# One FFN stage: the order of VectorE's weight-preparing operations within and across steps, and where a chunk's gating writes

## The chip, the cores and the metric

The program runs on one core of one Trainium2 chip. The metric is the device time of one execution in microseconds (us), smaller is better. The engines are named as in the profile: PE (TensorE, matrix products), DVE (VectorE, elementwise), ACT (ScalarE, elementwise and casts), POOL (GpSimd, here mostly the issuer of accumulating DMAs), SP (SyncE, the issuer of the plain loads).

## The reference

One decoder layer on 256 tokens of width 2048, all in float32: a half-weighted SwiGLU FFN, a token mixer, a second half-weighted FFN, a final norm.

```python
def swiglu(h, w_in, w_out):
    gu = h @ w_in
    gate, up = gu[..., :D_FF], gu[..., D_FF:]
    return (jax.nn.silu(gate) * up) @ w_out

h = h + 0.5 * swiglu(rmsnorm(h, ffn1_norm[l]), ffn1_w_in[l], ffn1_w_out[l])
...
h = h + 0.5 * swiglu(rmsnorm(h, ffn2_norm[l]), ffn2_w_in[l], ffn2_w_out[l])
return rmsnorm(h, final_norm)
```

D_FF is 5632. The change touches the two FFNs only; the mixer between them stays.

## The kernel before

**Numbers in two parts.** A float32 operand is held as a rounded part (`hi`, written by an ACT cast, L217) and the remainder (`lo`, written by a DVE subtraction, L220). One product of blocks is then three matmuls, hi x hi, hi x lo and lo x hi (`three`, L300).

**Chunks and steps.** The hidden width is cut into 11 chunks of 512. For each chunk a group of eight steps multiplies the rows by the chunk's gate and up columns; one step covers 256 rows of the weight, 1 MB, in four blocks of 512 columns. A step is of kind S (plain: 8 block products, 24 matmuls) or W (a scheme that trades one product for sums of blocks: 7 products, 21 matmuls). For W, POOL adds one weight block to another by an accumulating DMA (L265), and DVE forms two more sums in the step's own raw tile (`sums`, L273 to L282): the first is 128x512, the second 128x2x512 and needs the first. `KINDS` (L62) gives the kinds by chunk; chunks 3 to 10 are all SWWWWWWW.

**What a W step asks of DVE.** Five operations: the lower part of its three plain blocks (`lo_b`, 128x1536), the first sum (128x512), the second sum (128x1024), and the lower parts of the pairs u and t (`lo_t`, each 128x1024). ACT casts the same parts ahead of each. An S step has one lower part, 128x2048; the first step of a closing group has it as two halves.

**Tiles.** Raw weights lie in a ring of four tiles (three in `ring_raw`, one in `fring_raw` or `zring_raw`); the load of a step waits until the step four before has been read for the last time. Split blocks come from 21 places, 12 for S steps and for the pairs u and t, 9 for the W steps' plain blocks; a place is free again when PE has used it.

**Order.** In `middle` the instructions of DVE, ACT and PE stand in the order in which the program writes them. Its list of phases names, for each step k, what is prepared in which order: casts and load of step k+1 (`hi_b`), lower part of k (`lo_b`), both sums of k, casts of u and t (`hi_t`), lower parts of u and t (`lo_t`). `prepare` runs ahead along this list as far as free places allow, then PE's next unit (half a step) is written. The first chunk of an FFN (`opening`) and the last group (`closing`) are ordered by the framework's scheduler.

**Between chunks.** W products are collected in two PSUM tiles `pw`. At a chunk's end `combine` (L430) turns them into two SBUF tiles `add` by one ACT copy and four DVE operations (L440 to L443). One unit later (`GATE_AT`) `gate` adds them into the chunk's PSUM sums (L628), and forms silu(gate) x up into two buffers of the pool `tmp` (L635 on ACT, L637 on DVE). Two units later (`TURN_AT`) `turned` transposes the result on PE (L648) and splits it (L653, L654). Then a closing group of mostly four S steps, `w_out` times the hidden values of two chunks, runs into PSUM tiles that share their banks with `pw`; `put_away` adds its result to rows in DRAM by POOL DMAs (L685). `x_rows` (L825) loads the input rows for the norm's statistics.

Of the kernel before, what the change touches and what calls it, by code (L numbers as in the profile page):

```python
# [36 lines left out]
P = 128  # L37
# [25 lines left out]
    "f": ("SSSSSSSS", "SSSSSSSS", "WWSWWWSS") + CHUNKS,  # L63
    "z": ("SSSSSSSS", "SWSWWWSS", "WWSWWWSS") + CHUNKS,
# [13 lines left out]
T_BLOCKS = 12  # L78
STRIDE = {"t": 2, "b": 3}
# [7 lines left out]
def layer(ctx: ExitStack, tc: tile.TileContext, io):  # L87
# [7 lines left out]
    tmp = ctx.enter_context(tc.tile_pool(name="tmp", bufs=2))  # L95
# [136 lines left out]
    class Step:  # L232


        def __init__(self, kind, src, halves=False):
            self.kind, self.src, self.halves = kind, src, halves
# [21 lines left out]
        def hi_b(self):  # L258
# [5 lines left out]
            if self.kind == "W":  # L264
                nc.gpsimd.dma_start(  # L265
                    out=self.raw[:, 0, :], in_=self.src[:, CW : 2 * CW], accum_op=ALU.add
                )
            self.hi("b", *((3, "b") if self.kind == "W" else (4, "t")))

        def lo_b(self):  # L270
            self.lo("b")

        def sums(self):  # L273
            if self.kind != "W":
                return
            w = self.raw

            def tt(out, x, y, op):
                nc.vector.tensor_tensor(out=out, in0=x, in1=y, op=op)  # L279
# [4 lines left out]
        def hi_t(self):  # L284
            if self.kind == "W":
                self.hi("u", 2, "t")
                self.hi("t", 2, "t")

        def lo_t(self):
            if self.kind == "W":  # L290
                self.lo("u")
                self.lo("t")
# [284 lines left out]
    def ffn(psum, spool, act, pair, w_in, w_out, row, name, finish, first=None, behind=None):  # L577
# [26 lines left out]
        def opening(c):  # L604
            kinds = KINDS[name][c]
            grp = group(kinds, f"{name}i{c}")
            for i, (kind, kp) in enumerate(pairs_of(c)):
                early = first and c == 0
                if early:
                    act(2 * kp)  # L610
                b = s_step(w_in[c, kp], 4 if early and i == 0 else 2 if early and i == 1 else 1)
                if early:
                    first(kp + 1)
                grp.s(a_of(kp), b)
                if i >= S_AT:
# [5 lines left out]
            a_t = gate(c, grp)  # L621
            turned(c, grp, a_t)

        def gate(c, grp):

            for t in range(NT):
                if grp.with_w:
                    nc.vector.tensor_tensor(  # L628
                        out=grp.acc[t], in0=grp.acc[t], in1=grp.add[t], op=ALU.add
                    )  # L630
            a_t = []
            for t in range(NT):
                r = rstd[0][:, t : t + 1]
                s = tmp.tile([P, CW], F32, tag="sil", name=f"{name}s{c}_{t}")
                nc.scalar.activation(out=s, in_=grp.acc[t][:, 0, :], func=AF.Silu, scale=r)  # L635
                a = tmp.tile([P, CW], F32, tag="act", name=f"{name}a{c}_{t}")
                nc.vector.scalar_tensor_tensor(  # L637
                    out=a, in0=grp.acc[t][:, 1, :], scalar=r, in1=s, op0=ALU.mult, op1=ALU.mult,
                )
                a_t.append(a)  # L640
            return a_t
# [48 lines left out]
        def middle(groups):  # L690

            steps, plan = [], []
            for g in groups:
                if isinstance(g, int):
                    mine = [
                        (Step(kind, w_in[g, kp]), a_of(kp), kp if kind == "W" else None)
# [17 lines left out]
            later = []  # L714

# [22 lines left out]

            k = 0
            for g, mine in plan:  # L740
# [13 lines left out]
                if isinstance(g, int):  # L754
                    def close_up(g=g, grp=grp):
                        a_t = gate(g, grp)
                        later.append([TURN_AT, lambda: turned(g, grp, a_t)])

                    later.append([GATE_AT, close_up])
# [5 lines left out]
        opening(0)  # L765
        with tc.manual_schedule(engines=IN_ORDER):
            grp = middle(GROUPS[1:-1])
# [584 lines left out]
```

## Time and profile before

| | us |
|---|---|
| three runs | 1724.27, 1724.39, 1727.79 |
| median | 1724.39 |
| the profiled execution | 1726.89 |
| its span, first to last instruction | 1725.1 |
| granted clock of PE in it, share of full | 0.996 |

The profile describes one execution. Busy time is listed by engine; matmuls overlap, so their ends are modelled and a busy PE is not PE at its peak. A row of the timeline gives start, length, engine, line, operation, what it writes and reads, its shape and count, and in square brackets idle time of that engine just before and what ended it. A row of the waits gives who waited for whom: us in total, how many times, the longest. A row of the stretches gives the stretch, its length, and for PE, PE's weight loads, DVE, ACT and POOL the busy us with the count of instructions, then the granted clock, the DMA engines' busy share and GB/s.

### The profile page before, as it was taken

To read this page: it belongs to the slowest core of one execution; us is meant where nothing else is said; L and a number is where in the kernel's file an instruction comes from. 1 tells how busy PE (TensorE), PEld (TensorE's weight loads), DVE (VectorE), ACT (ScalarE), POOL (GpSimd) and SP (SyncE) were. 2 spreads that over 40 slices of the span, in tenths; PEclk is the share of its full clock that TensorE was granted. 3 is DMA by queue.
4 is the path that set the end of the run, shared out by engine and by line. 5 is a ranking of instruction groups with operands and counts; after the bars stand their busy time and mean duration, and the time that the engine had idled before them with its cause. 6 is when DMAs were issued, how large, how long until landed. Compare 5 with 4: busy or idle time off the path is not lost. (4 is left out here: it accounts for less than half of the span.)

```text
span 1725.1 us, 21190 instructions
## 1 busy us (share of the span) xinstructions
PE 1686.3 (98%) x7657; PEld 1394.0 (81%) x7657; DVE 1428.5 (83%) x1353; ACT 1011.7 (59%) x1231; POOL 174.6 (10%) x196
## 2 busy tenths in 40 slices
PE   9999999999999999999999999999999999999997
PEld 7888887887887787888988887888878878878876
DVE  8678999999999997645454677889999999999984
ACT  7565566566666564563454555556656666666553
POOL 0010110011011010000000000101101101101112
PEclk9999999999999999999999999999999999999999
DMA  9777897887897796554665666878879878978972
GB/s 347 267 223 235 242 252 236 246 256 237 241 261 236 227 299 222 187 180 140 201 202 180 202 217 174 223 237 243 248 227 256 257 227 240 271 221 254 261 267 93
DMA packets 123387, 398.36 MB, mean 231 GB/s; under 512 B 13825, under 2 KB 17025, under 8 KB 123282
## 3 DMA queue, kind: packets, MB, share of 16 engines
q1 hardware_dynamic: 97026, 335.63, 57.5%
q0 software_dynamic: 25536, 60.30, 18.3%
q8 instruction: 60, 0.98, 0.2%
q10 hardware_dynamic: 720, 1.07, 0.2%
q14 instruction: 45, 0.37, 0.1%
HBM read 371.78 MB, written 25.17 MB: 230 GB/s over the span
## 5 line engine op out<-in xcount | busy, mean ns | idle before, releaser
L217 ACT CAST ring_hi<-ring_raw 128x1024 fp32r<-128x1024 f32 (+3 forms) x558 | 552.4, 1014 | 379.8 <-issue 78.3
L220 DVE TENSOR_TENSOR ring_lo<-ring_raw,ring_hi 128x1024 fp32r<-128x1024 f32 (+5 forms) x443 | 633.7, 1446 | 156.2 <-ACT ring_hi L217 153.6
L279 DVE TENSOR_TENSOR ring_raw<-ring_raw 128x512 f32<-128x512 f32 (+1 forms) x178 | 170.6, 959 | 24.1 <-DMA ring_raw<-in_ffn_w_in 18.4
L303 PE MATMUL ps_fo<-ring_hi,fhi 128*128 128x512 f32 x352 | 138.8, 395 | 9.0 <-DVE add_fi L440 9.0
L265 POOL DMA_DIRECT2D ring_raw<-in_ffn_w_in x89 | 77.1, 866 | 695.8 <-DMA ring_raw<-in_ffn_w_in 349.7
L303 PE MATMUL ps_zo<-ring_hi,zhi 128*128 128x512 f32 x344 | 135.6, 395 | 9.6 <-DVE add_zi L440 9.6
L303 PE MATMUL ps_fo<-ring_hi,flo 128*128 128x512 f32 x352 | 137.2, 390 | 0.0
L303 PE MATMUL ps_fo<-ring_lo,fhi 128*128 128x512 f32 x352 | 137.2, 390 | 0.0
L303 PE MATMUL ps_zo<-ring_hi,zlo 128*128 128x512 f32 x344 | 133.9, 390 | 0.0
L303 PE MATMUL ps_zo<-ring_lo,zhi 128*128 128x512 f32 x344 | 133.8, 389 | 0.0
L303 PE MATMUL pw_zi<-ring_hi,s_z 128*128 128x512 f32 x390 | 131.1, 390 | 1.7 <-DVE zlo L654 1.6
L303 PE MATMUL pw_fi<-ring_hi,s_f 128*128 128x512 f32 x366 | 122.8, 389 | 0.0
L303 PE MATMUL ps_fi<-ring_hi,xT_hi 128*128 128x512 f32 x282 | 109.3, 392 | 2.0 <-ACT ring_hi L217 2.0
L303 PE MATMUL ps_fi<-ring_lo,xT_hi 128*128 128x512 f32 x282 | 110.5, 392 | 0.2 <-DVE ring_lo L220 0.2
L303 PE MATMUL ps_fi<-ring_hi,xT_lo 128*128 128x512 f32 x282 | 110.2, 391 | 0.0
L217 ACT CAST ring_hi<-zring_raw 128x1024 fp32r<-128x1024 f32 x82 | 80.2, 1003 | 38.8 <-DVE zring_raw L279 23.4
L303 PE MATMUL ps_zi<-ring_hi,h_lo 128*128 128x512 f32 x255 | 99.4, 390 | 0.0
L303 PE MATMUL ps_zi<-ring_hi,h_hi 128*128 128x512 f32 x255 | 99.3, 389 | 0.0
L303 PE MATMUL ps_zi<-ring_lo,h_hi 128*128 128x512 f32 x255 | 99.2, 389 | 0.0
L220 DVE TENSOR_TENSOR ring_lo<-zring_raw,ring_hi 128x1024 fp32r<-128x1024 f32 (+2 forms) x60 | 91.8, 1539 | 6.3 <-ACT ring_hi L217 6.2
L217 ACT CAST ring_hi<-fring_raw 128x1024 fp32r<-128x1024 f32 x72 | 71.5, 1015 | 35.2 <-issue 13.4
L220 DVE TENSOR_TENSOR ring_lo<-fring_raw,ring_hi 128x1024 fp32r<-128x1024 f32 (+2 forms) x54 | 81.4, 1518 | 12.2 <-ACT ring_hi L217 11.7
(307 smaller groups left out, 3484.9 us busy)
## 6 DMA issues: line engine op xcount, KB each, us to landing
ring_raw<-in_ffn_w_in SPq DMA_DIRECT2D x262, 512.0 KB, 6.4
ring_raw<-in_ffn_w_out SPq DMA_DIRECT2D x136, 512.0 KB, 5.0
ring_raw<-in_ffn_w_in POOLq DMA_DIRECT2D x89, 256.0 KB, 6.9
fring_raw<-in_ffn_w_in SPq DMA_DIRECT2D x44, 512.0 KB, 6.0
zring_raw<-in_ffn_w_in SPq DMA_DIRECT2D x44, 512.0 KB, 6.2
ring_raw<-in_w_out_mix SPq DMA_DIRECT2D x32, 512.0 KB, 3.8
fring_raw<-in_ffn_w_out SPq DMA_DIRECT2D x20, 512.0 KB, 5.0
zring_raw<-in_ffn_w_out SPq DMA_DIRECT2D x20, 512.0 KB, 4.6
```

What stands on the lines that cost most here:

```text
L217: nc.scalar.copy(out=hi[:, j:k, :], in_=src[:, j:k, :])
L220: nc.vector.tensor_tensor(out=lo, in0=src, in1=hi.bitcast(F32), op=ALU.subtract)
L265: nc.gpsimd.dma_start(out=self.raw[:, 0, :], in_=self.src[:, CW : 2 * CW], accum_op=ALU.add)
L279: nc.vector.tensor_tensor(out=out, in0=x, in1=y, op=op)
L303: nc.tensor.matmul(ps, x, y, start=start and i == 0, stop=stop and i == 2, **kw)
```

## The change

Eight edits, all in the FFN code.

- The phases become a table, `PHASES`: for each k the first sum of k, the cast of u of k, the lower part of t of step k-1, the second sum of k, the cast of t of k, casts and load of step k+2, the lower part `lo_b` of k+1, the lower part of u of k. `sums`, `hi_t` and `lo_t` are split accordingly. The list runs from k = -2. Casts of u and of t now ask for two free places each instead of four at once.
- PE's second unit of a W step is written once both `lo_u` and `lo_t` of it have been.
- `KINDS`: in the first FFN chunk 2 gets six W steps instead of five; in the second FFN chunks 1 and 2 keep four and five in other places.
- `gate` no longer adds into PSUM: it adds PSUM and `add` into `add`, and writes silu and the product over it. A chunk without W steps takes two such tiles anew.
- `opening` returns its group; `middle` gates chunk 0 eight units (first FFN) or one unit (second FFN) into chunk 1 and transposes two units later. Chunk 1 is gated at once instead of one unit later.
- `TMP_BUFS`: the pool `tmp` has one buffer of each tag instead of two.
- `x_rows` puts its rows into the pool `gpool` instead of the `add` tiles.
- `UNSENT` is empty: every W step still uses POOL's accumulating DMA.

```diff
-    "f": ("SSSSSSSS", "SSSSSSSS", "WWSWWWSS") + CHUNKS,
-    "z": ("SSSSSSSS", "SWSWWWSS", "WWSWWWSS") + CHUNKS,
+    "f": ("SSSSSSSS", "SSSSSSSS", "SWWWWWWS") + CHUNKS,
+    "z": ("SSSSSSSS", "SSWWWWSS", "SWWWWWSS") + CHUNKS,
...
+FIRST_GATE_AT = {"f": 8, "z": 1}
+UNSENT = {"f": (), "z": ()}
+TMP_BUFS = 1
+PHASES = (
+    ("sum_u", 0), ("cast_u", 0), ("lo_t", -1), ("sum_t", 0), ("cast_t", 0), ("cast_b", 2),
+    ("lo_b", 1), ("lo_u", 0),
+)
...
-    tmp = ctx.enter_context(tc.tile_pool(name="tmp", bufs=2))
+    tmp = ctx.enter_context(tc.tile_pool(name="tmp", bufs=TMP_BUFS))
...
         def need(self, phase):
-            w = self.kind == "W"
-            return {"hi_b": ("b", 3) if w else ("t", 4), "hi_t": ("t", 4 if w else 0)}.get(phase)
+            if phase == "cast_b":
+                return ("b", 3) if self.kind == "W" else ("t", 4)
+            return ("t", 2) if phase in ("cast_u", "cast_t") else None
...
-            tt(w[:, 2, :], w[:, 0, :], w[:, 2, :], ALU.subtract)
-            tt(w[:, 1:4:2, :], w[:, 1:4:2, :], w[:, 2:3, :].broadcast_to([P, 2, CW]), ALU.subtract)
+            self.less(self.raw[:, 2, :], self.raw[:, 0, :], self.raw[:, 2, :])
...
+            self.less(
+                w[:, 1:4:2, :], w[:, 1:4:2, :], w[:, 2:3, :].broadcast_to([P, 2, CW])
+            )
...
-            for t in range(NT):
-                if grp.with_w:
-                    nc.vector.tensor_tensor(
-                        out=grp.acc[t], in0=grp.acc[t], in1=grp.add[t], op=ALU.add
-                    )
+            if grp.with_w:
+                held = grp.add
+                for t in range(NT):
+                    nc.vector.tensor_tensor(out=held[t], in0=grp.acc[t], in1=held[t], op=ALU.add)
...
-                s = tmp.tile([P, CW], F32, tag="sil", name=f"{name}s{c}_{t}")
-                nc.scalar.activation(out=s, in_=grp.acc[t][:, 0, :], func=AF.Silu, scale=r)
-                a = tmp.tile([P, CW], F32, tag="act", name=f"{name}a{c}_{t}")
+                src = held[t] if grp.with_w else grp.acc[t]
+                s, a = held[t][:, 0, :], held[t][:, 1, :]
+                nc.scalar.activation(out=s, in_=src[:, 0, :], func=AF.Silu, scale=r)
...
-            for k in range(-1, len(steps)):
-                phases += [("hi_b", k + 1), ("lo_b", k), ("sums", k), ("hi_t", k), ("lo_t", k)]
-            phases = [(p, k) for p, k in phases if 0 <= k < len(steps)]
+            for k in range(-2, len(steps) + 1):
+                phases += [(phase, k + ahead) for phase, ahead in PHASES]
+            phases = [
+                (p, k) for p, k in phases
+                if 0 <= k < len(steps) and (steps[k].kind == "W" or p in ("cast_b", "lo_b"))
+            ]
...
-                    prepare(place["lo_t" if i and steps[k].kind == "W" else "lo_b", k])
+                    prepare(max(place[x, k] for x in (("lo_u", "lo_t") if i and steps[k].kind == "W" else ("lo_b",))))
...
+            close_later(0, before, FIRST_GATE_AT[name])
...
-                    later.append([GATE_AT, close_up])
+                    close_later(g, grp, 0 if g == 1 else GATE_AT)
...
-                rows = ftmp[0].tile([P, 2 * CW], F32, tag=f"add{t}", name=f"x_{np_}{t}")
+                rows = gpool.tile([P, 2 * CW], F32, tag=("g_hi", "g_lo")[t], name=f"x_{np_}{t}")
```

Lines move: L220 of before is L227 of the change, L279 is L306, L440 to L443 are L454 to L457, L628 is L642, L637 is L653, L648 is L663, L654 is L669, L303 is L317.

The order on DVE, first place: the second FFN's chunk 10, from the lower part of its second W step's plain blocks on, before. A 128x1536 row is `lo_b`, 128x512 the first sum, 128x2x512 the second, 128x1024 a lower part of u or t; `zring_raw` is the fourth raw tile, here the third W step's.

```order
L220 TENSOR_TENSOR zring_lo<-ring_raw,zring_hi 128x1536
L279 TENSOR_TENSOR ring_raw<-ring_raw 128x512
L279 TENSOR_TENSOR ring_raw<-ring_raw 128x2x512
L220 TENSOR_TENSOR ring_lo<-ring_raw,ring_hi 128x1024 x2
L220 TENSOR_TENSOR ring_lo<-zring_raw,ring_hi 128x1536
L279 TENSOR_TENSOR zring_raw<-zring_raw 128x512
L279 TENSOR_TENSOR zring_raw<-zring_raw 128x2x512
L220 TENSOR_TENSOR ring_lo<-zring_raw,ring_hi 128x1024 x2
```

And in the change:

```order
L227 TENSOR_TENSOR zring_lo<-ring_raw,zring_hi 128x1536
L227 TENSOR_TENSOR ring_lo<-ring_raw,ring_hi 128x1024
L306 TENSOR_TENSOR ring_raw<-ring_raw 128x512
L227 TENSOR_TENSOR ring_lo<-ring_raw,ring_hi 128x1024
L306 TENSOR_TENSOR ring_raw<-ring_raw 128x2x512
L227 TENSOR_TENSOR ring_lo<-zring_raw,ring_hi 128x1536
L227 TENSOR_TENSOR ring_lo<-ring_raw,ring_hi 128x1024
L306 TENSOR_TENSOR zring_raw<-zring_raw 128x512
L227 TENSOR_TENSOR ring_lo<-ring_raw,ring_hi 128x1024
L306 TENSOR_TENSOR zring_raw<-zring_raw 128x2x512
```

Each step's five operations stood together, first sum, second sum, u, t; now a lower part of the step before or after stands between the two sums and ahead of each first sum, and t of a step comes behind the next step's first sum.

Second place, DVE at the end of the same chunk, before: the seventh W step, whose raw tile is `zring_raw`, then the halves of the closing group's first step (from `ring_raw`) and `combine`.

```order
L220 TENSOR_TENSOR zring_lo<-zring_raw,zring_hi 128x1536
L279 TENSOR_TENSOR zring_raw<-zring_raw 128x512
L279 TENSOR_TENSOR zring_raw<-zring_raw 128x2x512
L220 TENSOR_TENSOR ring_lo<-zring_raw,ring_hi 128x1024 x2
L220 TENSOR_TENSOR ring_lo<-ring_raw,ring_hi 128x1024 x2
L440 TENSOR_TENSOR add_zi_1_11341<-pw_zi_0_11126,add_zi_0_11340 128x512
L441 TENSOR_TENSOR add_zi_0_11340<-pw_zi_1_11127,add_zi_1_11341 128x512
```

And in the change, from the lower part of the seventh step's plain blocks on:

```order
L227 TENSOR_TENSOR zring_lo<-zring_raw,zring_hi 128x1536
L227 TENSOR_TENSOR ring_lo<-ring_raw,ring_hi 128x1024
L306 TENSOR_TENSOR zring_raw<-zring_raw 128x512
L227 TENSOR_TENSOR ring_lo<-ring_raw,ring_hi 128x1024
L306 TENSOR_TENSOR zring_raw<-zring_raw 128x2x512
L227 TENSOR_TENSOR ring_lo<-ring_raw,ring_hi 128x1024 x2
L227 TENSOR_TENSOR ring_lo<-zring_raw,ring_hi 128x1024 x2
L454 TENSOR_TENSOR add_zi_1_11267<-pw_zi_0_11050,add_zi_0_11266 128x512
L455 TENSOR_TENSOR add_zi_0_11266<-pw_zi_1_11051,add_zi_1_11267 128x512
```

The two halves of the closing group's first step (the two rows of 128x1024 from `ring_raw` ahead of the last pair) stood behind the seventh step's u and t, and now stand ahead of them; `combine` follows the same set of operations in both.

Third place, PE in the second FFN's chunk 1, from the last transposes of chunk 0 (`ztp`) to the first matmul into the second `pw` tile (`pw_zi_1`), which takes the bank that the transposes held. Before:

```order
L648 MATMUL ztp_7338<-ident,za_1_7336 128x128 x4
L303 MATMUL ps_zi_0_7355<-ring_hi,h_lo_6422 128x512
L303 MATMUL ps_zi_0_7355<-ring_hi,s_z_7147 128x512
L303 MATMUL ps_zi_0_7355<-ring_lo,s_z_7147 128x512
L303 MATMUL ps_zi_0_7355<-ring_hi,s_z_7147 128x512
L303 MATMUL pw_zi_0_7420<-ring_hi,h_hi_6418 128x512
L303 MATMUL pw_zi_0_7420<-ring_lo,h_hi_6418 128x512
L303 MATMUL pw_zi_0_7420<-ring_hi,h_lo_6422 128x512
L303 MATMUL pw_zi_0_7420<-ring_hi,s_z_7147 128x512
L303 MATMUL pw_zi_0_7420<-ring_lo,s_z_7147 128x512
L303 MATMUL pw_zi_0_7420<-ring_hi,s_z_7147 128x512
L303 MATMUL pw_zi_1_7421<-ring_hi,s_z_7147 128x512
```

And in the change:

```order
L663 MATMUL ztp_7377<-ident,zg_0_7343 128x128 x4
L663 MATMUL ztp_7377<-ident,zg_1_7344 128x128 x4
L317 MATMUL ps_zi_0_7296<-ring_hi,h_hi_6383 128x512
L317 MATMUL ps_zi_0_7296<-ring_lo,h_hi_6383 128x512
L317 MATMUL ps_zi_0_7296<-ring_hi,h_lo_6387 128x512
...
L317 MATMUL pw_zi_0_7404<-ring_hi,s_z_7111 128x512
L317 MATMUL pw_zi_0_7404<-ring_lo,s_z_7111 128x512
L317 MATMUL pw_zi_0_7404<-ring_hi,s_z_7111 128x512
L317 MATMUL pw_zi_1_7405<-ring_hi,s_z_7111 128x512
```

Ten matmuls stood between, now 24 do (the rows left out are matmuls of chunk 1).

More of the change, by code (lines that the diff above doesn't have):

```diff
@@ L268, in hi_b, with cast_u, cast_t, lo_u @@
             self.hi("b", *((3, "b") if self.kind == "W" else (4, "t")))
+        def cast_u(self):
+            self.hi("u", 2, "t")
+        def cast_t(self):
+            self.hi("t", 2, "t")
         def lo_b(self):
             self.lo("b")
-        def sums(self):
-            if self.kind != "W":
-                return
-            w = self.raw
-            def tt(out, x, y, op):
-                nc.vector.tensor_tensor(out=out, in0=x, in1=y, op=op)
-            tt(w[:, 2, :], w[:, 0, :], w[:, 2, :], ALU.subtract)
-            tt(w[:, 1:4:2, :], w[:, 1:4:2, :], w[:, 2:3, :].broadcast_to([P, 2, CW]), ALU.subtract)
[L284 to L292, printed above, removed]
+        def lo_u(self):
+            self.lo("u")
+        def lo_t(self):
+            self.lo("t")
+        def sum_u(self):
+            if not self.sent:
+                q = self.raw[:, 0, :]
+                nc.vector.tensor_tensor(out=q, in0=q, in1=self.raw[:, 1, :], op=ALU.add)
+            self.less(self.raw[:, 2, :], self.raw[:, 0, :], self.raw[:, 2, :])
+        def sum_t(self):
+            w = self.raw
+            self.less(
+                w[:, 1:4:2, :], w[:, 1:4:2, :], w[:, 2:3, :].broadcast_to([P, 2, CW])
+            )
+        def less(self, out, x, y):
+            nc.vector.tensor_tensor(out=out, in0=x, in1=y, op=ALU.subtract)
         def __getitem__(self, key):
@@ L695, in middle @@
                     mine = [
-                        (Step(kind, w_in[g, kp]), a_of(kp), kp if kind == "W" else None)
+                        (
+                            Step(kind, w_in[g, kp], sent=g not in UNSENT[name]),
+                            a_of(kp), kp if kind == "W" else None,
+                        )
                         for kind, kp in pairs_of(g)
@@ L714, in middle, with close_later, close_up @@
             later = []
+            def close_later(g, grp, when):
+                def close_up():
+                    a_t = gate(g, grp)
+                    later.append([TURN_AT, lambda: turned(g, grp, a_t)])
+                if when:
+                    later.append([when, close_up])
+                else:
+                    close_up()
             def prepare(upto):
```

31 lines of the change are left out of this document (15 added, 16 removed).

## The prediction

> **What bounds the kernel now.** I read four views in this order: the page's busy time, busy time by stretch, the waits of the matrix engine, and the timeline of one chunk.
>
> ```profile
> PE 1686.3 (98%) x7657; PEld 1394.0 (81%) x7657; DVE 1428.5 (83%) x1353; ACT 1011.7 (59%) x1231; POOL 174.6 (10%) x196
> 75.00:211.00 136.00, 135.59 (x611) 112.14 (x609) 114.49 (x95) 82.66 (x94) 14.06 (x16) 1.00 0.76 224
> 211.00:656.00 445.00, 434.59 (x1929) 356.36 (x1930) 423.65 (x360) 277.83 (x316) 56.60 (x65) 1.00 0.85 250
> 1213.00:1659.00 446.00, 434.29 (x1926) 355.85 (x1927) 423.89 (x359) 278.19 (x316) 62.74 (x68) 1.00 0.85 251
> ```
>
> PE's 98% and DVE's 83% are averages. The first number after each stretch's length is PE, the third DVE. In the two long stretches (chunks 3 to 10 of either FFN) DVE is busy 95% and PE idles 10.4 and 11.7 us; before 211 us PE hardly idles and DVE has 21.5 us to spare. So only the two long stretches can gain much, and what ends PE's waits there matters:
>
> ```profile
> PE ps_zo L303 <- DVE add_zi L440: 9.6, 8, 1.7
> PE ps_fo L303 <- DVE add_fi L440: 9.0, 8, 1.3
> PE pw_zi L303 <- DVE ring_lo L220: 2.5, 4, 1.2
> PE pw_fi L303 <- DVE ring_lo L220: 1.8, 4, 0.8
> PE pw_zi L303 <- DVE zlo L654: 1.6, 1, 1.6
> DVE ring_raw L279 <- DMA ring_raw<-in_ffn_w_in: 18.4, 11, 2.6
> ...
> 273.59 0.40 PE L303 MATMUL ps_fi<-ring_hi,xT_lo 128*128 128x512 f32 x1
> 275.22 0.49 PE L303 MATMUL ps_fo<-ring_hi,fhi 128*128 128x512 f32 x1 [1.23 <-DVE add_fi L440]
> 275.55 0.39 PE L303 MATMUL ps_fo<-ring_lo,fhi 128*128 128x512 f32 x1
> 275.78 0.40 PE L303 MATMUL ps_fo<-ring_hi,flo 128*128 128x512 f32 x1
> ```
>
> All large waits of PE are for DVE: sixteen for L440 (one for each of these chunks, before the closing group may take the sums' bank), eight for lower parts, one for the first chunk of the second FFN. They are 24.5 us. Matmuls start 0.23 us apart here, and the one at 275.22 started 1.63 after its forerunner: 1.40 lost where 1.23 is shown, so 25 waits cost some 4.2 more, 28.7 in all. Nothing done to DVE in these stretches can bring more. DVE itself waits 11 times for the accumulate that a W step's first sum needs.
>
> Chunk 4 of the first FFN on DVE (its seven W steps are W1 to W7, the closing group's first step S1):
>
> ```profile
> 229.76 1.95 DVE L279 TENSOR_TENSOR fring_raw<-fring_raw 128x512 f32<-128x512 f32 x2
> 231.70 2.43 DVE L220 TENSOR_TENSOR ring_lo<-fring_raw,ring_hi 128x1024 fp32r<-128x1024 f32 x2
> 234.05 1.75 DVE L220 TENSOR_TENSOR fring_lo<-ring_raw,fring_hi 128x1536 fp32r<-128x1536 f32 x1
> 237.71 1.95 DVE L279 TENSOR_TENSOR ring_raw<-ring_raw 128x512 f32<-128x512 f32 x2 [1.91 <-DMA ring_raw<-in_ffn_w_in]
> 239.58 2.49 DVE L220 TENSOR_TENSOR ring_lo<-ring_raw,ring_hi 128x1024 fp32r<-128x1024 f32 x2
> 241.98 1.75 DVE L220 TENSOR_TENSOR fring_lo<-ring_raw,fring_hi 128x1536 fp32r<-128x1536 f32 x1
> ...
> 267.93 1.95 DVE L279 TENSOR_TENSOR ring_raw<-ring_raw 128x512 f32<-128x512 f32 x2
> 269.87 4.69 DVE L220 TENSOR_TENSOR ring_lo<-ring_raw,ring_hi 128x1024 fp32r<-128x1024 f32 x4
> 274.48 0.68 DVE L440 TENSOR_TENSOR add_fi<-pw_fi,add_fi 128x512 f32<-128x512 f32 x1
> 275.26 0.69 DVE L441 TENSOR_TENSOR add_fi<-pw_fi,add_fi 128x512 f32<-128x512 f32 x1
> 275.86 0.68 DVE L442 TENSOR_TENSOR add_fi<-pw_fi,add_fi 128x512 f32<-128x512 f32 x1
> 276.58 0.69 DVE L443 TENSOR_TENSOR add_fi<-pw_fi,add_fi 128x512 f32<-128x512 f32 x1
> ```
>
> W1's sums stand at 229.76, W2's at 237.71 behind the 1.91 us wait, W7's at 267.93: 30.22 us for five steps, 6.04 each. From 237.71 to L440 at 274.48 DVE does not pause: 36.77 us.
>
> **The change, part by part.** *The order of DVE's operations (term A).* What is alternation worth? L442 needs L440's result, with L441 between: it starts 0.60 after L441, which takes 0.69, so 0.08 early. L443 needs L442's result directly before it: it starts 0.72 after, 0.04 late. One operation in between is worth 0.12 us.
>
> The Trainium skill speaks against this: "VectorE: DVE Perf Modes", sections "The DRAIN you can't avoid" and "Rules for kernel authors", says a flush follows every operation whether or not semaphores chain it, so only fewer operations help. By that rule the cycle stays at 6.04 and the change loses time (third rival); the L441 to L443 rows disagree. Its section "Two Vector instructions with no wait between them", by which an unheld instruction starts early, agrees with them.
>
> A W step is five operations:
>
> ```profile
> L220 DVE TENSOR_TENSOR ring_lo<-ring_raw,ring_hi 128x1024 fp32r<-128x1024 f32 x84 | 101.0, 1222 | 2.3 <-ACT ring_hi L217 1.4
> L279 DVE TENSOR_TENSOR ring_raw<-ring_raw 128x1024 f32<-128x1024 f32 x35 | 42.9, 1225 | 1.2
> L279 DVE TENSOR_TENSOR ring_raw<-ring_raw 128x512 f32<-128x512 f32 x35 | 24.2, 692 | 9.4 <-DMA ring_raw<-in_ffn_w_in 8.4
> L220 DVE TENSOR_TENSOR ring_lo<-ring_raw,ring_hi 128x1536 fp32r<-128x1536 f32 x12 | 21.0, 1752 | 0.0
> ```
>
> They sum to 0.69 + 1.23 + 2 x 1.22 + 1.75 = 6.11; the measured 6.04 means that early and late starts nearly cancel. With all five 0.083 early the step takes 5.70, **0.34 less**, 2.4 in seven steps. But the new order also moves work. The t lower part of W1 now stands behind W2's first sum, so behind the DMA wait, and S1's lower parts (two halves) now stand ahead of W7's u and t. From W2's first sum to the first operation of `combine` the new sequence is 5 x 5.70 = 28.5, then one 0.61 and six of 1.14 (W6's t, W7's second sum, S1's halves, W7's u and t), 7.45: 35.98 in place of 36.77. PE needs W7's t only four matmuls (0.9) before the closing group, about as long as `combine`'s first operation (0.68), so PE's start follows this chain as before. The part queued behind W2's wait is in time: PE takes W1's t some 3.9 us into W1, and six more W steps of 4.8 (21 x 0.23) end at 273.8, which puts that need near 243; the part is ready at 239.6. A chunk whose W2 waits for the DMA thus gains 0.8, not 2.4. The waits' row counts 11 such chunks: 8.8. The first chunk of each stretch had DVE ahead and gains 2.4 each: 4.8. The other three lie between 0.8 and 0.8 + 1.2 + 0.34 = 2.3; the landing had under 0.8 to spare in them, so I take 1.1: 3.3. **A = 16.9.** All of it is DVE's path, which PE follows while it still waits; 28.7 is there to take.
>
> *Casts two steps ahead, tiles freed later (term B).* A step's raw tile comes free with its t lower part, and the load four steps on waits for that.
>
> ```profile
> 234.16 0.83 SPq L185 DMA_DIRECT2D fring_raw<-in_ffn_w_in  x2
> 242.09 6.80 SPq L185 DMA_DIRECT2D ring_raw<-in_ffn_w_in  x4
> 304.68 7.09 SPq L185 DMA_DIRECT2D ring_raw<-in_ffn_w_in  x4
> ...
> 237.06 2.03 POOL L685 DMA_DIRECT2D hd<-half_f  x2
> 240.97 0.88 POOL L265 DMA_DIRECT2D fring_raw<-in_ffn_w_in  x1 [1.88 <-DVE ring_lo L220]
> 250.13 0.87 POOL L265 DMA_DIRECT2D ring_raw<-in_ffn_w_in  x1 [8.29 <-DVE ring_lo L220]
> 316.00 0.87 POOL L265 DMA_DIRECT2D ring_raw<-in_ffn_w_in  x1 [10.65 <-DVE ring_lo L220]
> ...
> fring_raw<-in_ffn_w_in POOLq DMA_DIRECT2D x1, 256.0 KB, 10.7
> ring_raw<-in_ffn_w_in POOLq DMA_DIRECT2D x1, 256.0 KB, 5.5
> ring_raw<-in_ffn_w_in POOLq DMA_DIRECT2D x1, 256.0 KB, 7.1
> ```
>
> The last three rows are times from issue to landing of the accumulates issued at 240.97, 250.13 and 316.00. W6's load went out at 242.09, 4.38 after W2's first sum; it was needed four cycles after that sum: 24.2 - 4.4 = 19.8 us allowed. Load and accumulate took until 250.13 + 5.5: 13.5. In chunk 5 they took from 304.68 to 316.00 + 7.1: 18.4. Afterwards the tile is free one cycle plus a sum and a lower part (5.70 + 1.85) after its own sum, and allowed is 4 x 5.70 - 7.55 = **15.3**. Of the 14 chunks behind the first ones, W6 takes over 15.3 in five, by 6.7 us together. The load moves later into a calmer time, or just shifts: nothing or all 6.7; I take **B = -3.5**. W7's load has the same allowance; S1's needs no accumulate. On ACT the cast two steps ahead now stands ahead of the next step's u cast and holds it when its load is late, but ACT is busy only 278 of 445 us, and the u part on DVE comes four operations after its sum.
>
> *Step kinds (term D).* The first FFN's chunk 2 has six W steps for five: 21 matmuls for 24, 3 x 0.23 = **0.7 gained**. DVE's work grows there by 6.0 less an S step's lower part (two halves, 2.4): 3.6, hidden by the 21.5 us that it idles before 211; without this cover PE would wait those 3.6. In the second FFN the counts stay.
>
> *First chunk's gating (term C).* In the second FFN PE waited 1.6 (1.8 with the restart) for L654, the last reader of the transposes' bank. After, 24 matmuls (5.4 us) stand between the transposes and the matmul that takes that bank, where 10 stood: **1.8 gained**, nothing at worst. In the first FFN gating moves 8 units later, and its result is first used behind 16 units; PE's 135.59 of 136 there says nothing waited.
>
> *Gating in the sums' tiles; one temporary buffer; x rows in another pool.* Gating has as many operations of the same shapes; a sum into SBUF takes 1225 ns (L279) and PE waits for none of these but through DVE. A single buffer and the moved rows act in the openings, where DVE has slack; I bound them at 2 us either way, nothing taken.
>
> The sum: 16.9 - 3.5 + 0.7 + 1.8 = 15.9. The profiled execution took 1726.89 for a span of 1725.1; it becomes about 1711.0. The runs' median, 1724.39, is 2.5 lower, so I forecast **1708.5**.
>
> **The rivals.** *All waits go (1695).* If DVE's gain outruns PE everywhere, 28.7 + 0.7 = 29.4 go. For it: 28.7 over 16 chunks is only 1.8 us a chunk. Against: W2's DMA wait eats the moved lower part. Chance 0.14.
>
> *Given back (1719 to 1728).* B at its end of 6.7, `combine` held up by casts waiting for loads two steps ahead, an opening 2 us longer: 16.9 + 2.5 - 6.7 - 2 leaves 10.7; a W2 landing another 0.5 later in 14 chunks leaves 3.7, that is 1721. Chance 0.12.
>
> *Alternation gains nothing (1735).* If the flush behind each operation cannot be hidden, the cycle stays at 6.04 and only the moved lower part counts: 1.2 in each of 11 chunks is 13.2 lost, less 2.5: 1724.4 + 10.7. The L442 row speaks against it. Chance 0.04. This is what the Trainium skill's rule above would make of the change.
>
> *The raw tiles become the bound (slower, 1743).* W5's load and accumulate now take from 234.16 to 240.97 + 10.7, 17.5 us, since its accumulate queues behind the two row transfers of 237.06. After the change W5's load leaves later still, behind W2's sum at about 239.6. If it takes 18 there, DVE waits 18 - 15.3 = 2.7 in each of 14 chunks: 38 lost against 16.9 + 2.5 gained, 18.6 slower. The point that decides is 15.3 + 19.4/14 = 16.7 us. Against: leaving at 239.6 it resembles today's W6 (242.09, 13.5 us), with the row transfers ahead of it for less time. Chance 0.08.
>
> **How the numbers follow.** The forecast's own case (1700 to 1719) has 0.62. A measurement of this kernel tells 0.2%, 3.4 us, from no change. Faster by more: 0.62 + 0.14 + a third of the given-back case (0.04) = 0.80. Within 0.2%: 0.08. Slower: 0.04 + 0.08 = 0.12. The range 1694 to 1722 leaves out the two slow cases and the upper half of the given-back one, 0.18 in all.
>
> **What would show it.** In the changed profile the W steps' cycle on DVE should read 5.70 from first sum to first sum; 6.04 means that alternation gains nothing. PE's waits for the first operation of `combine` should shrink and partly move to `pw` waiting for the lower parts of W6 and W7, since S1's halves stand ahead. DVE's waits for the accumulate before W2 should grow by about 1 us each; waits before W5 or W6 beyond 1 us mean the raw tiles bind. The wait on the second FFN's first transposes should be gone. The forecast is wrong if W2's accumulate lands sooner than today (then more is gained) or W5's lands later.

## The result, and the profile after

| | before | after |
|---|---|---|
| median of six runs each, us | 1725.18 | 1734.82 |
| range of the runs | 1718.44 to 1728.11 | 1731.34 to 1741.21 |
| ratio, 95% interval | | 1.0065 (1.0038 to 1.0092) |
| the profiled execution | 1726.89 | 1731.34 |
| its span | 1725.1 | 1729.6 |

The change is 0.65% slower, where 0.9% faster was forecast. The profiled execution is the fastest of the six, so the two profiles show 4.5 us of the loss where the medians show 9.6.

The page's busy times and the stretches of the changed kernel (columns as before the change):

```profile
PE 1694.3 (98%) x7654; PEld 1389.6 (80%) x7654; DVE 1407.1 (81%) x1357; ACT 1015.6 (59%) x1233; POOL 176.8 (10%) x197
75.00:211.00 136.00, 135.95 (x611) 112.23 (x611) 115.62 (x100) 83.19 (x95) 14.90 (x17) 1.00 0.81 235
211.00:656.00 445.00, 433.63 (x1904) 350.01 (x1903) 406.94 (x352) 273.56 (x311) 56.73 (x65) 1.00 0.86 244
1213.00:1659.00 446.00, 437.79 (x1925) 354.04 (x1925) 411.85 (x358) 277.76 (x315) 58.55 (x66) 1.00 0.86 248
```

DVE is busy 21.4 us less in all and 91 to 92% instead of 95% in the long stretches, yet PE does not get through them sooner. The waits of DVE and PE say where DVE's time went (who waited for whom: us in total, how many times, the longest):

```profile
DVE ring_raw L306 <- DMA ring_raw<-in_ffn_w_in: 34.0, 16, 3.1
DVE zring_lo L227 <- ACT zring_hi L224: 12.8, 8, 2.8
DVE fring_raw L306 <- DMA fring_raw<-in_ffn_w_in: 7.1, 5, 2.4
...
PE pw_fi L317 <- DVE ring_lo L227: 11.5, 20, 1.5
PE pw_zi L317 <- DVE ring_lo L227: 8.7, 16, 0.8
```

DVE's waits for accumulates grew from 18.4 us in 11 places to 41.1 in 21; `fring_raw`, W5's tile in the first FFN, is new among them. PE's sixteen waits for `combine` are gone, but it stops 36 times for a lower part instead, 20.2 us (before: eight times, 4.3 us).

The timeline of chunk 5 of the first FFN on DVE, from W2's first sum:

```profile
297.74 0.69 DVE L306 TENSOR_TENSOR ring_raw<-ring_raw 128x512 f32<-128x512 f32 x1 [2.78 <-DMA ring_raw<-in_ffn_w_in]
298.35 1.22 DVE L227 TENSOR_TENSOR ring_lo<-fring_raw,ring_hi 128x1024 fp32r<-128x1024 f32 x1
...
312.62 1.76 DVE L227 TENSOR_TENSOR ring_lo<-fring_raw,ring_hi 128x1536 fp32r<-128x1536 f32 x1 [0.56 <-ACT ring_hi L224]
314.30 1.22 DVE L227 TENSOR_TENSOR ring_lo<-ring_raw,ring_hi 128x1024 fp32r<-128x1024 f32 x1
317.12 0.69 DVE L306 TENSOR_TENSOR fring_raw<-fring_raw 128x512 f32<-128x512 f32 x1 [1.61 <-DMA fring_raw<-in_ffn_w_in]
...
322.81 0.68 DVE L306 TENSOR_TENSOR ring_raw<-ring_raw 128x512 f32<-128x512 f32 x1
323.41 1.22 DVE L227 TENSOR_TENSOR ring_lo<-fring_raw,ring_hi 128x1024 fp32r<-128x1024 f32 x1
...
328.49 0.69 DVE L306 TENSOR_TENSOR ring_raw<-ring_raw 128x512 f32<-128x512 f32 x1
...
336.30 0.69 DVE L454 TENSOR_TENSOR add_fi<-pw_fi,add_fi 128x512 f32<-128x512 f32 x1 [0.32 <-ACT add_fi L453]
```

Where nothing waits, first sums follow each other by 5.68 (322.81 to 328.49), as forecast; but W5 waited twice, for its cast and for its accumulate, and from W2's first sum to `combine` it took 38.56.

A chunk is a loop, and two lengths make it up: from the first operation of `combine` to W2's first sum, and from there to the next `combine`. The table gives them as means over 14 chunks (4 to 10 of either FFN), read from such timeline rows of each kernel; the experiments' names stand in it already. (e3 has one more DVE operation in every W step and is left out.)

| kernel | `combine` to W2 | W2 to `combine` | sum |
|---|---|---|---|
| before | 26.45 | 37.05 | 63.50 |
| the change | 26.26 | 37.87 | 64.12 |
| e1, old order | 26.28 | 36.99 | 63.27 |
| e2, order alone | 26.46 | 37.88 | 64.34 |
| e4, change and fifth raw tile | 23.89 | 37.54 | 61.43 |
| e5, old order and fifth raw tile | 25.13 | 37.56 | 62.68 |
| e6, t in its own step | 25.99 | 37.61 | 63.60 |
| e7, change without rows | 26.02 | 36.43 | 62.45 |
| e8, halves last | 25.98 | 37.38 | 63.36 |
| e9, before without rows | 25.99 | 37.20 | 63.19 |
| e10, rows late | 26.02 | 37.38 | 63.40 |
| e11, halves last, rows late | 26.31 | 37.42 | 63.72 |
| e12, halves last, no rows | 26.35 | 36.00 | 62.35 |

The first length is a chain of transfers behind DVE's operations, and alternation cannot shorten it: W2's load waits for the lower part of the closing group's third step, then come load and accumulate. In the chunk above:

```profile
270.94 0.69 DVE L454 TENSOR_TENSOR add_fi<-pw_fi,add_fi 128x512 f32<-128x512 f32 x1 [0.32 <-ACT add_fi L453]
...
279.66 2.29 DVE L227 TENSOR_TENSOR ring_lo<-ring_raw,ring_hi 128x2048 fp32r<-128x2048 f32 x1
282.01 7.32 SPq L192 DMA_DIRECT2D ring_raw<-in_ffn_w_in  x6
288.47 0.86 POOL L273 DMA_DIRECT2D ring_raw<-in_ffn_w_in  x1 [7.05 <-DMA ring_raw<-in_ffn_w_in]
```

The tile is free at 281.95, the load leaves at 282.01, the accumulate at 288.47, and W2's sum starts at 297.74, 26.80 after `combine`.

### The profile page after: what moved, and what is told of

Same layout as the page of the kernel before. It is cut to its first block, busy times and chain, and to the rows that moved or that the text cites. A ratio compares the mean times of both kernels' runs of the same rounds, so it can differ in the third digit from the quotient of the medians.

```text
span 1729.6 us, 21218 instructions
## 1 busy us (share of the span) xinstructions
PE 1694.3 (98%) x7654; PEld 1389.6 (80%) x7654; DVE 1407.1 (81%) x1357; ACT 1015.6 (59%) x1233; POOL 176.8 (10%) x197
## 3 DMA queue, kind: packets, MB, share of 16 engines
q0 software_dynamic: 25680, 60.57, 19.1%
## 4 chain that ended last, share of the span: by engine, by line
PE 55%; DMA 17%; DVE 16%; issue 9%; ACT 1%; POOL 0%; DVEq 0%; SPq 0%; POOLq 0%; ACTq 0%
DMA ring_raw<-in_ffn_w_in 14%; PE ps_fo L317 8%; DVE ring_lo L227 8%; PE ps_zo L317 8%; PE ps_zi L317 8%; PE ps_fi L317 7%; PE ps_h L317 5%; DVE ring_raw L306 4%; PE pw_zi L317 4%; DMA fring_raw<-in_ffn_w_in 3%; PE ps_mp L317 3%; PE ps_mv L317 3%; PE pw_fi L317 2%; PE ps_mg L317 2%; PE ps_mq L317 1%
## 5 line engine op out<-in xcount | busy, mean ns | idle before, releaser
L227 DVE TENSOR_TENSOR ring_lo<-ring_raw,ring_hi 128x1024 fp32r<-128x1024 f32 (+5 forms) x445 | 632.7, 1437 | 137.4 <-ACT ring_hi L224 137.3
L306 DVE TENSOR_TENSOR ring_raw<-ring_raw 128x512 f32<-128x512 f32 (+1 forms) x182 | 173.4, 953 | 34.5 <-DMA ring_raw<-in_ffn_w_in 34.0
L317 PE MATMUL ps_fo<-ring_hi,fhi 128*128 128x512 f32 x352 | 137.8, 392 | 0.0
L317 PE MATMUL ps_fo<-ring_hi,flo 128*128 128x512 f32 x352 | 137.2, 390 | 0.0
L317 PE MATMUL ps_fo<-ring_lo,fhi 128*128 128x512 f32 x352 | 137.1, 389 | 0.0
L317 PE MATMUL ps_zo<-ring_hi,zhi 128*128 128x512 f32 x344 | 134.6, 392 | 0.0
L317 PE MATMUL ps_zo<-ring_hi,zlo 128*128 128x512 f32 x344 | 133.8, 389 | 0.0
L317 PE MATMUL ps_zo<-ring_lo,zhi 128*128 128x512 f32 x344 | 133.7, 389 | 0.0
L317 PE MATMUL pw_zi<-ring_hi,s_z 128*128 128x512 f32 x390 | 131.1, 390 | 0.0
L317 PE MATMUL pw_fi<-ring_hi,s_f 128*128 128x512 f32 x372 | 125.1, 390 | 0.0
L317 PE MATMUL ps_fi<-ring_hi,xT_hi 128*128 128x512 f32 x275 | 107.4, 394 | 1.3 <-ACT ring_hi L224 1.3
L317 PE MATMUL ps_fi<-ring_lo,xT_hi 128*128 128x512 f32 x275 | 107.7, 392 | 0.2 <-DVE ring_lo L227 0.2
L317 PE MATMUL ps_fi<-ring_hi,xT_lo 128*128 128x512 f32 x275 | 107.6, 391 | 0.0
L317 PE MATMUL ps_zi<-ring_hi,h_hi 128*128 128x512 f32 x247 | 96.2, 390 | 0.0
L317 PE MATMUL ps_zi<-ring_hi,h_lo 128*128 128x512 f32 x247 | 96.2, 390 | 0.0
L317 PE MATMUL ps_zi<-ring_lo,h_hi 128*128 128x512 f32 x247 | 96.2, 389 | 0.0
L227 DVE TENSOR_TENSOR ring_lo<-zring_raw,ring_hi 128x1024 fp32r<-128x1024 f32 (+2 forms) x58 | 89.1, 1549 | 5.6 <-ACT ring_hi L224 5.6
L317 PE MATMUL pw_zi<-ring_lo,s_z 128*128 128x512 f32 x195 | 79.4, 407 | 9.4 <-DVE ring_lo L227 8.7
```

The lines of the kernel that those rows point to most:

```text
L227: nc.vector.tensor_tensor(out=lo, in0=src, in1=hi.bitcast(F32), op=ALU.subtract)
L306: nc.vector.tensor_tensor(out=out, in0=x, in1=y, op=ALU.subtract)
L317: nc.tensor.matmul(ps, x, y, start=start and i == 0, stop=stop and i == 2, **kw)
```

## The experiments

The experiments ran on four chips, each time beside the kernel before, which took 1721 to 1722 us there. So each is read by its ratio to before, beside the change's 1.0065 (which is 1733 there). That ratio comes from the pair above; its interval alone, 0.27% or 4.6 us either way, goes into every difference to the change.

The expectations name two theories of the loss. Theory 1a: raw tiles come free later, and what waits for their transfers costs the time. Theory 1b: PE's stops for lower parts cost it, whatever the DMAs do.

**e1 and e2: the order, and the rest.** e1 puts the old phases back:

```diff
+    ("cast_b", 1), ("lo_b", 0), ("sum_u", 0), ("sum_t", 0), ("cast_u", 0), ("cast_t", 0),
+    ("lo_u", 0), ("lo_t", 0),
-    ("sum_u", 0), ("cast_u", 0), ("lo_t", -1), ("sum_t", 0), ("cast_t", 0), ("cast_b", 2),
-    ("lo_b", 1), ("lo_u", 0),
```

> The changed kernel with the phases of before put back (casts one step ahead, a step's five VectorE operations together); step kinds, gating in the sums' tiles, late first gating, single buffers and the moved x rows stay. Theory 1, the loss sits in the new order: this is before less the small terms (0.7 for the sixth W step, 1.8 for the transposes), 1722, and PE again waits some 9 us in either FFN for the first operation of combine. Theory 2, the loss sits in the other edits: this stays near the changed kernel, 1735.

> The kernel before with the new phases alone; step kinds, gating into PSUM, two temporary buffers and x rows as before. Theory 1 (the order loses): about 1737, with the accumulate's waits on VectorE near the 41 us of the changed kernel where before has 18.6. Theory 2 (the other edits lose): about 1710, the gain that was predicted for the order.

e1 took 1721.01, ratio 0.9993 (0.9984 to 1.0001); e2 1746.49, ratio 1.0137 (1.0121 to 1.0154). The loss is the order's. The other edits are worth some 1.4 us under the old order, which the interval does not tell from none, but some 12 under the new one, which alone loses twice as much: in e2, PE stops once for 5.1 us at the second FFN's first transposes, a stop that the change has not.

**e3: no accumulates.** `UNSENT` lists chunks 1 to 10, so the first addition of each W step runs on DVE.

> The changed kernel with every W step's first addition on VectorE (UNSENT lists all chunks from 1 on), so no accumulating DMA on the weights: 0.69 more VectorE work for each of 7 steps, a cycle of about 6.3, and no wait for an accumulate. Theory 1a, the later raw tiles and the accumulate's latency cost the time: the 41 us of waits fall below 10, each chunk pays 4.3 and gets back up to 4, so 1730 to 1745. Theory 1b, the price is PE's waits for lower parts, whatever the DMAs do: the 4.3 a chunk come on top, 1765 or more.

1760.92, ratio 1.0226 (1.0212 to 1.0239), between the two expectations. DVE is busy 444.4 of 456 us in the first FFN's long stretch and becomes the bound, so this run says only that the additions cost more than the waits they remove; it does not tell the theories apart.

**e4 and e5: a fifth raw tile, with either order.**

```diff
-MORE_RAW = 1
+MORE_RAW = 2
...
-            src = tmp.tile([P, 2, T], F32, tag="act", name=f"sa_{name}{kp}")
+            src = gpool.tile([P, 4, T], F32, tag="g_lo", name=f"sa_{name}{kp}")[:, :2, :]
```

> The changed kernel with a fifth raw tile (the room comes from a temporary buffer whose place the gating's pool gives in the openings), so a load may leave one step earlier, some 5.7 us. Theory 1a (raw tiles freed later): VectorE's 41 us of waits for the accumulate fall to under 10 and the time to 1700 to 1712. Theory 1b (PE waits for lower parts because of the order): the DMA waits fall, but PE's waits for lower parts stay near 20 us and the time at 1728 or above.

> Old phases, all other edits, and the fifth raw tile: the fourth corner beside the old order (1721.0), the changed kernel (1734.8) and the changed kernel with a fifth tile (1691.6). If the tiles are what the new order lacks and alternation itself is worth 0.34 a W step, the old order gains only its own 18 us of accumulate waits: 1703, still bound by a VectorE cycle of 6.04. Rival, the tile does everything and alternation nothing: 1692.

e4 took 1691.61, ratio 0.9823 (0.9809 to 0.9836); e5 1713.66, ratio 0.9949 (0.9937 to 0.9962). The tile alone is worth 7 us under the old order, less than either expectation: DVE waits for no accumulate there any more, but its loop still takes 62.68 a chunk. With the tile the new order is worth 22, and e4 is faster than theory 1a expected. e4's stretch and two steps of its chunk 5:

```profile
211.00:640.00 429.00, 429.00 (x1922) 355.80 (x1921) 410.70 (x356) 277.54 (x315) 55.80 (x64) 1.00 0.87 257
...
270.22 0.69 DVE L454 TENSOR_TENSOR add_fi<-pw_fi,add_fi 128x512 f32<-128x512 f32 x1 [0.87 <-ACT add_fi L453]
275.28 6.83 SPq L192 DMA_DIRECT2D ring_raw<-in_ffn_w_in  x4
...
294.11 0.68 DVE L306 TENSOR_TENSOR ring_raw<-ring_raw 128x512 f32<-128x512 f32 x1
```

PE does not pause once. W2's load leaves among the four issues from 275.28 on, and its sum starts 23.89 after `combine` with no wait before it; every one of the 14 chunks takes 61.4, which is PE's own time (267 matmuls, 0.23 apart). The fifth tile does not take the rows away, it covers them: now W6's load leaves beside them, and load and accumulate take 17.9 on average over the 14 chunks, but land at least 2.1 before W6's sum. Of the kernels that leave nothing out e4 is the fastest.

**e6: another alternating order with four raw tiles.** The phases become first sum of k, plain lower part of k+1, second sum of k, u of k, t of k:

```diff
+    ("sum_u", 0), ("cast_u", 0), ("lo_b", 1), ("sum_t", 0), ("cast_t", 0), ("cast_b", 2),
+    ("lo_s", 1), ("lo_u", 0), ("lo_t", 0),
```

`lo_s` is the lower part of an S step that is not halved.

> Four raw tiles, another alternating order: first sum of k, plain lower part of k+1, second sum, u, t, so a raw tile is free with its own step, 5.7 us after its first sum instead of 7.6, W1's t no longer stands behind W2's wait, and the halves of the closing group's first step stand between W7's sums. Theory 1a (tiles freed late and what stands behind the waits): the accumulate waits fall from 41 to about 20 and the time to 1700 to 1718. Rival, two casts ahead or gating cost the time: 1735 as the change.

1727.54, ratio 1.0030 (1.0019 to 1.0041), between the two expectations. The waits for accumulates did fall to 12.6 us, but the time only by 6 us, little more than the uncertainty of the change's ratio: DVE now waits 19.5 us for the copy ahead of `combine`, and PE still 19.1 for lower parts. A tile freed sooner helps; this order buys it with other waits.

**e7 and e9: the rows of the closing groups.** Both leave out the `dma_start` in `put_away`, so two row transfers behind each closing group.

> The changed kernel without the two row transfers that put_away gives to POOL behind each closing group (the rows in DRAM miss those parts, so the output lacks them). Theory 1a with the collision: W5's accumulate lands 3 to 5 earlier, its 7 us of waits go, W2's stay, 1722 to 1728. Rival, the row transfers only coincide: 1735.

> The kernel before without put_away's two row transfers (the rows in DRAM miss those parts, so the output lacks them): the control for the changed kernel without them, which gained 28 us. Theory (the rows hurt through W5's load, which only the new order sends out behind them): in before the stretch from W2's first sum to combine is 36.8 in most chunks whatever the rows do, and the stretch from combine to W2's sum is set by the load behind S3's lower part, so 1716 to 1722. Rival (the rows cost any order the same): 1694.

e7 took 1706.50, ratio 0.9909 (0.9895 to 0.9924), 27 us below the change by the ratios and more than either theory said; e9 1722.37, ratio 1.0003 (0.9989 to 1.0016). So the row transfers, the same bytes in both, cost the old order nothing that shows and the new one some 27 us. Chunk 5 of the change shows how, from POOL, SP and the transfers' times from issue to landing:

```profile
297.51 2.13 POOL L700 DMA_DIRECT2D hd<-half_f  x2
310.19 0.88 POOL L273 DMA_DIRECT2D fring_raw<-in_ffn_w_in  x1 [10.54 <-DVE ring_raw L306]
...
299.60 1.04 SPq L192 DMA_DIRECT2D fring_raw<-in_ffn_w_in  x2
...
hd<-half_f POOLq DMA_DIRECT2D x1, 512.0 KB, 11.2
fring_raw<-in_ffn_w_in SPq DMA_DIRECT2D x1, 512.0 KB, 10.0
...
fring_raw<-in_ffn_w_in POOLq DMA_DIRECT2D x1, 256.0 KB, 6.8
```

The rows leave at 297.51, W5's load at 299.60, beside them: a row transfer takes up to 11.2 us and the load's first half 10.0; the accumulate can leave at 310.19 and takes 6.8. Without rows (e7):

```profile
296.97 0.82 SPq L192 DMA_DIRECT2D fring_raw<-in_ffn_w_in  x2
...
303.88 0.86 POOL L273 DMA_DIRECT2D fring_raw<-in_ffn_w_in  x1 [7.14 <-DVE ring_raw L306]
...
fring_raw<-in_ffn_w_in SPq DMA_DIRECT2D x1, 512.0 KB, 6.1
...
fring_raw<-in_ffn_w_in POOLq DMA_DIRECT2D x1, 256.0 KB, 5.8
...
312.15 0.69 DVE L306 TENSOR_TENSOR fring_raw<-fring_raw 128x512 f32<-128x512 f32 x1
```

6.1 and 5.8, and W5's sum starts without a wait. Chunk 5 is no exception: over the 14 chunks the first half of W5's load takes 9.0 on average in the change and 5.1 in e7. In before, W5's load left at 234.16, ahead of the rows at 237.06, so only its accumulate stood behind them, and 19.8 us of allowance covered that.

**e8 and e12: the halves behind W7's u and t again.**

```diff
+    ("sum_u", 0), ("cast_u", 0), ("lo_t", -1), ("lo_h", 0), ("sum_t", 0), ("cast_t", 0),
+    ("cast_b", 2), ("lo_b", 1), ("lo_u", 0),
```

`lo_h` is the halved lower part of the closing group's first step; e12 leaves the row transfers out as well.

> The changed kernel with the two halved lower parts of the closing group's first step behind W7's u and t again, as before the change. Theory 1a: the same sum of work stands between W2's landing and combine, so 1735 within 4, with fewer of PE's waits for W7's lower parts and a wait for combine in their place. Theory 1b (PE's stops and restarts at lower parts are the price): 1725 to 1729.

> The changed kernel with the halves behind W7's u and t and without the two row transfers (the rows in DRAM miss those parts, so the output lacks them). What the halves' place is worth once no late load disturbs: with theory 1a only the clean stretch from W2's first sum to combine shrinks, from 36.20 to 35.96, 14 times 0.24 less than the 1706.5 without rows: 1703. Rival 1b, PE's stops at W7's lower parts cost some 12 us whatever the DMAs do: 1694.

e8 took 1722.10, ratio 1.0002 (0.9989 to 1.0015), by the ratios 11 us better than the change and below both expectations, which spoke for theory 1b. e12 took 1702.17, ratio 0.9884 (0.9868 to 0.9901): 4.3 better than e7, near theory 1a's 3.4 and not the 12 of 1b. The two intervals overlap, and the loops differ by only 0.10 a chunk, 1.4 us. So the halves' place is worth 4 us or less where no transfer disturbs. The chunk's end on DVE and PE in the change (second FFN, chunk 4) shows that part:

```profile
1274.40 2.36 DVE L227 TENSOR_TENSOR ring_lo<-ring_raw,ring_hi 128x1024 fp32r<-128x1024 f32 x2
1276.67 2.36 DVE L227 TENSOR_TENSOR ring_lo<-zring_raw,ring_hi 128x1024 fp32r<-128x1024 f32 x2
1279.34 0.69 DVE L454 TENSOR_TENSOR add_zi<-pw_zi,add_zi 128x512 f32<-128x512 f32 x1 [0.30 <-ACT add_zi L453]
...
1277.95 0.50 PE L317 MATMUL pw_zi<-ring_lo,s_z 128*128 128x512 f32 x1 [0.84 <-DVE ring_lo L227]
1279.68 0.39 PE L317 MATMUL pw_zi<-ring_hi,s_z 128*128 128x512 f32 x1
1280.60 0.39 PE L317 MATMUL ps_zo<-ring_hi,zhi 128*128 128x512 f32 x1
```

The halves (1274.40) hold W7's u back to 1276.67; PE stops for it until 1277.95, and DVE and ACT then wait for PE's products. In e8:

```profile
1266.78 2.50 DVE L227 TENSOR_TENSOR ring_lo<-zring_raw,ring_hi 128x1024 fp32r<-128x1024 f32 x2
1269.21 2.35 DVE L227 TENSOR_TENSOR ring_lo<-ring_raw,ring_hi 128x1024 fp32r<-128x1024 f32 x2
1271.48 0.69 DVE L461 TENSOR_TENSOR add_zi<-pw_zi,add_zi 128x512 f32<-128x512 f32 x1
```

`combine` follows the halves without a wait. Why e8 gains some 6 us more than that beside the row transfers was not settled: both lengths of its loop are shorter, by 0.28 and 0.49 a chunk, though its waits for accumulates are not (42.2 us in all). DVE's waits for casts behind W4's first sum are shorter: 7.6 us over the 14 chunks, in place of 12.1.

**e10 and e11: the rows moved instead of dropped.** The two issues come 13 units later, behind W7's accumulate; e11 adds the halves' place of e8.

```diff
+            def rows():
+                with tc.issue_after(last_sum[0]):
                     nc.gpsimd.dma_start(
...
+            later.append([ROWS_AFTER, rows])
```

> The changed kernel with both row transfers issued behind W7's accumulate instead of behind W4's; nothing is left out. Theory: W5's load no longer runs beside them, the stretch from W2's first sum to combine falls from 37.9 to about 36.3 a chunk, 14 times 1.6: 1710 to 1716. Rival (the transfers cost by their bytes, wherever they run, or now hold up the next combine that needs their tiles): 1725 to 1735.

> Rows behind W7's accumulate and the closing group's first step's halves behind W7's u and t. If the two act apart, 12.7 of the one and some 20 of the other add up: 1700 to 1706, below both kernels with four raw tiles, and each chunk is 26.2 from combine to W2's first sum plus 35.96 to the next combine, 62.2. If both removed the same waits: 1710 to 1716.

e10 took 1719.31, ratio 0.9989 (0.9970 to 1.0009), e11 1721.70, 0.9997 (0.9982 to 1.0012). e10 lies between its two expectations, e11 is slower than both of its. W5 no longer waits, but the transfers met other loads. ACT in e10, and the time of a half of the load it waits for:

```profile
332.93 1.05 ACT L226 CAST ring_hi<-fring_raw 128x1024 fp32r<-128x1024 f32 x1 [2.23 <-DMA fring_raw<-in_ffn_w_out]
334.19 1.05 ACT L226 CAST ring_hi<-fring_raw 128x1024 fp32r<-128x1024 f32 x1 [0.20 <-DMA fring_raw<-in_ffn_w_out]
335.14 0.58 ACT L455 COPY add_fi<-pw_fi 128x512 f32<-128x512 f32 x1
...
fring_raw<-in_ffn_w_out SPq DMA_DIRECT2D x1, 512.0 KB, 10.1
...
DVE add_fi L456 <- ACT add_fi L455: 13.8, 9, 1.9
DVE add_zi L456 <- ACT add_zi L455: 12.3, 10, 2.4
```

The closing group's second step now loads beside the rows, 10.1 us; its casts stand on ACT ahead of the copy that `combine` needs, and DVE waits up to 1.9 there in the first FFN and 2.4 in the second. About half of the collision's price came back in a new place, and e11's two gains did not add up.

## Why the prediction was wrong, point by point

**Alternation (A): the mechanism held.** The cycle is 5.68 for 5.70. From W2's first sum to `combine` 35.98 were forecast (the terms add up to 35.95). The change's own order takes 36.20 where nothing waits but `combine` (two chunks of the change, most of e7). With the halves last e12 takes 36.00, and its loop of 62.35 is before's 26.45 plus 35.98 within 0.1. Without the row transfers, which cost before nothing, the change gains 0.91% (e7), 15.7 us, and 1.16% with the halves last (e12), 20.0, where A, C and D had promised 19.4. The rival that alternation gains nothing is refuted: the row at 323.41 starts 0.08 before the sum of 322.81, 0.68 long, has ended. With it falls that reading of the Trainium skill's "VectorE: DVE Perf Modes", sections "The DRAIN you can't avoid" and "Rules for kernel authors", by which only fewer operations help; its section "Two Vector instructions with no wait between them" agrees with these rows.

**The step that failed is B,** the raw tiles freed later, taken at -3.5 with an end of -6.7, all of it for W6. The allowance of 15.3 held: in chunk 5 W5's load left at 299.60, and its sum was due three cycles behind W2's, at 314.8, so 15.2 later. What was mis-sized is the time that W5's load and accumulate take. The trace of the change gives it from issue to landing for the 14 chunks: 16.1 on average, over 15.3 in ten of them, by 17.0 us together; W6's and W7's are over it by 1.1 and 1.3. So in its own terms B comes to some -19, and 17.0 of that is W5's, which the sum had at nothing. In e7, without the rows, W5's time is 11.5 on average and never over 15.3. The mis-sized place is the one that the slower rival named and that got a chance of 0.08. It was set aside with "it resembles today's W6 (242.09, 13.5 us), with the row transfers ahead of it for less time". But the rows leave with the end of the closing group, 0.23 before W2's first sum in chunk 5, and the load 1.86 behind that sum, so it runs its whole way beside them: from 299.60 to 317.03, where the sum is let go, 17.4 us. The prediction's own sign for this, waits before W5 beyond 1 us, is in the profile (2.4 at the longest).

B also set aside the casts ("ACT is busy only 278 of 445 us"). The lower part of W5's plain blocks stands ahead of W5's sum and needs their cast, which needs the load alone:

```profile
311.01 1.57 ACT L224 CAST ring_hi<-fring_raw 128x1024 fp32r<-128x1024 f32 x2 [3.54 <-DMA fring_raw<-in_ffn_w_in]
```

Over the 14 chunks DVE waited for such a cast in nine, 12.1 us, and for W5's accumulate in five, 7.1 us, all of these in the first FFN. Eight of the nine casts had waited for the load; at one the trace names PE. In e7 all of these waits are gone.

In the lengths of the loop the same is seen. In the change the second length is 1.89 a chunk above 35.98, 26.5 us in 14 chunks: 1.44 a chunk, 20.2 us, goes with the row transfers (37.87 to 36.43 in e7), and 0.43, 6.0 us, with the halves ahead of W7's u (36.43 to 36.00 in e12, though there 0.33 comes back in the first length). The rival's price was 2.7 a chunk; 1.44 puts W5's case at the rival's own point of decision, 16.7. The rows alone eat the 19.4 that A, C and D had promised, and with 6.0 for the halves the change is 6.8 slower by this sum. The pair shows 9.6, between 6.6 and 15.9; the rest stays open.

**A smaller step failed with it:** "PE's start follows this chain as before". PE needs W7's u first, and from it twelve matmuls to the closing group. With the halves ahead, PE stops for W7's u in each of the 14 chunks (0.8 in thirteen of them), its closing group starts 1.26 after `combine` where before has 0.74, and `combine` itself waits 0.3.

**Right:** the waits for W2's accumulate grew, as forecast, from 18.4 to 31.5 us over the 14 chunks, so that even a clean chunk keeps only some 0.6 to 0.8 of what alternation saves. The wait for the second FFN's first transposes (C) is gone. C and D together were put at 2.5; under the old order all edits but the order gave 1.4 (e1), not told from none. That they would be worth 12 under the new order was not foreseen, and why was not settled beyond the one stop of 5.1 us in e2.

## What to carry to other kernels

An engine that is 95% busy in a stretch can still stand in a loop, here one of 63.5 us a chunk, whose other half is a chain of transfers (26.5): take the loop apart by the two events at which it closes, and ask of each half what a faster engine shortens. An operation that is moved later frees its buffer later, and then the question is not only how long the next load takes but beside which transfer it now leaves; look up the issue times of both. Give the new order the buffer it needs before judging it: with four raw tiles it lost 0.65%, with five it won 1.8%.

## What the runs showed of the hardware

In this kernel a plain load that leaves beside accumulating row transfers takes far longer: 10.0 us for 512 KB in chunk 5 where the same load takes 6.1 without them (9.0 and 5.1 on average over 14 chunks), and 10.1 for another load that they met in e10. The same transfers, with the same bytes, cost nothing that shows in the old order (ratio 1.0003 without them) and some 27 us in the new one: their price hangs on which load leaves beside them, not on their bytes alone.

On DVE an operation that does not need the one directly before it starts 0.08 us before that one's end (323.41 against 323.49), and five operations a step take 5.68 so in place of 6.04.
